# A hybrid decoder layer on one core: the last gate's first 128 channels projected inside the last stick-breaking head, a second PSUM bank for that head's values, and two products moved from GpSimd to VectorE

## The chip, the cores and the metric

The kernel runs on one core of a Trainium2 chip. The metric is the device time of one execution in microseconds (us); lower is better. The kernel before was timed in three runs: 560.47, 561.9 and 562.62 us, median 561.9.

## The reference

One layer over 1024 tokens and 1024 channels, in float32. `h` is the normalised input; one matrix product gives all projections, and three groups of heads work on their columns:

```python
proj = h @ w_in
(mu, mv, mi, mf, mz, aq, ak, av, az, sq, sk, sv, sz) = jnp.split(proj, OFFSETS, axis=-1)
y_m = mlstm_branch(...) * silu(mz)                        # 4 heads of 96, 384 columns
y_a = swa_branch(aq, ak, av, a_sinks) * silu(az)          # 6 heads of 64, 384 columns
y_s = stickbreak_branch(sq, sk, sv) * silu(sz)            # 4 heads of 64, 256 columns
y = concat([y_m, y_a, y_s]) @ w_out
x = x + gate * rmsnorm(y, g_post)
```

Stick-breaking attention, per head, for query t and keys s < t:

```python
z = q @ k.T * S_DH ** -0.5
a[t, s] = sigmoid(z[t, s]) * prod(sigmoid(-z[t, r]) for r in s+1 .. t-1)
out = a @ v
```

## The kernel before

Every float32 matrix product is made of three products of rounded parts (high by high, high by low, low by high). `hh` and `hl` hold the two parts of the transposed normalised input, 8 tiles of 128 channels by 1024 tokens. A projection of 128 channels is 48 matmuls: two halves of 512 tokens, each 3 times 8 (class `ProjD`, line 359, tile `pd<item>_<half>`). Items of this kind lie in one list, the filler. `fill(n, until)` issues the next n of its matmuls on TensorE and stops at item `until`; so the filler's matmuls stand between those of the attention stages. Items 10 to 12 are the gates `mz` (pd8 to pd10), 13 to 15 the gates `az` (pd11 to pd13), and the last four the gate `sz` of the stick-breaking heads: pd14 half 0, pd15 half 0, pd14 half 1, pd15 half 1. Each gate is multiplied with its group's output: ScalarE takes the sigmoid of the PSUM bank (L471), VectorE multiplies bank and output (L473), GpSimd multiplies in the sigmoid (L484). For `mz` and `az` the result is split in two parts and stored to DRAM (`d_yh`, `d_yl`); for `sz` it is kept in `ys`, and its split into tiles 6 and 7 of `hh`/`hl` is deferred (`late`), since the projections still read `hh`.

Order of stages, as the order on TensorE is written in the program: input, mLSTM, sliding-window attention (SWA, 8 tiles of 128 queries), stick-breaking (heads 0 to 3), the rest of the filler, the output projection. The order on the other engines is made by a scheduler at build time. Both are fixed sequences per engine: an instruction that waits holds up all behind it on its engine.

A stick-breaking head is cut in 12 pieces z (128 queries by up to 512 keys). `s_z`: TensorE writes z to one of three PSUM banks in turn (L964, L965, for the diagonal also L967), ScalarE makes sigmoid(z) into `sg` (L970) and sigmoid(-z) in place (L972), VectorE scans it to the running product `pr` (L981), and the product `sg*pr` (L983) goes to GpSimd where the piece is wider than 256, else to VectorE. A bank is free for the third piece after it when its scan has read it. `s_t` transposes the products on TensorE (L995, tile `tp`), ScalarE and VectorE split them in `ah` and `al` (L70, L71), and `s_pv`, three steps later, multiplies by the values (L1013, L1014) into one PSUM bank `ops` per four query tiles (a quad), which ScalarE and VectorE empty into `ys` (L1019, L1020). A head has 10 steps (pairs of query tiles by pairs of key tiles); after each step the filler gets 6.6 matmuls on average. In the code up to item `I_SZ` = 16, so none of `sz`.

After the last head, `wo_load(k)` loads 128 rows of the output weights (512 KB) and splits them into `woh` and `wol` (ScalarE, then GpSimd or VectorE), with two buffers for the loaded rows; `y_load(n)` loads the six stored tiles of half n over `hh`/`hl`, and the output projection goes through k = 0 to 7, for the first four token tiles (24 matmuls each k).

Of the kernel before, what the change touches and what calls it, by code (L numbers as in the profile page):

```python
# [13 lines left out]
ALU = mybir.AluOpType  # L14
# [7 lines left out]
NT = 8  # L22
# [4 lines left out]
SH = 4  # L27
# [11 lines left out]
AF_ = (4, 5, 4)  # L39
# [7 lines left out]
def trunk(ctx: ExitStack, tc, x, w_ss, w_gate, rows, cols, w_mu, w_mif, w_dm, w_av, wqk, bif, alibi, w_out,  # L47
          out):
    nc = tc.nc
    V, A, G, T = nc.vector, nc.scalar, nc.gpsimd, nc.tensor  # L50
# [12 lines left out]
    def load(dst, src):  # L63
        nc.sync.dma_start(f32(dst), f32(src))
# [3 lines left out]
    def split(dst_h, dst_l, src, e_hi, e_lo):  # L68

        e_hi(dst_h, src)  # L70
        e_lo.tensor_tensor(out=dst_l, in0=src, in1=dst_h.bitcast(F32), op=ALU.subtract)  # L71
# [41 lines left out]
    hh = hp.tile([P, KT, S], F32R, name="hh")  # L113
    hl = hp.tile([P, KT, S], F32R, name="hl")
# [331 lines left out]
        A.copy(v97[:, i, :, 0:MD], ps[:, 0:384].rearrange("p (h d) -> p h d", h=MH))  # L446
        A.copy(igf[:, :, 4 * i:4 * i + 4], ps[:, 384:392].rearrange("p (a h) -> p a h", a=2))  # L447

    late, due, clock = [], {}, [0]

    def later(n, f):

        due.setdefault(clock[0] + n, []).append(f)

    def tick():
        clock[0] += 1
        for f in due.pop(clock[0], ()):
            f()


    def from_dram(d, j):
        def src(n, t):
            z = gst.tile([P, 512], F32, tag="ymr", bufs=3, name=f"{d.name}r{j}_{n}")
            load(z, d[j, :, t])
            return z
        return src

    def gated(dst_j, name):
        def f(ps, n, t, src):
            sg = gst.tile([P, 512], F32, tag="gs", bufs=2, name=f"gs_{name}{n}")  # L470
            A.activation(sg, ps, AF.Sigmoid)  # L471
            y = src
            V.tensor_tensor(out=y, in0=ps, in1=src, op=ALU.mult)  # L473

            def rest():
                if dst_j >= 6:
                    late.append(lambda: split(hh[:, dst_j, t], hl[:, dst_j, t], y, A.copy, V))
                    return
                h = stg.tile([P, 512], F32R, tag="sh", bufs=2, name=f"sh_{name}_{n}")
                l = stg.tile([P, 512], F32R, tag="sl", bufs=2, name=f"sl_{name}_{n}")  # L480
                split(h, l, y, A.copy, G)
                store(d_yh[dst_j, :, t], h)
                store(d_yl[dst_j, :, t], l)
            later(1, lambda: G.tensor_tensor(out=y, in0=y, in1=sg, op=ALU.mult))  # L484
            later(2, rest)
        return f

    fill = Filler([ProjT(w_mif, MIF, "mif", evac_mif), ProjD(7, evac_hl(d_akh, d_akl, 0, 1.0, "ak")),
                   ProjT(w_av, AVSV, "av", evac_v)]
                  + [ProjD(4 + j, evac_hl(d_aqh, d_aql, j, 0.125, "aq")) for j in range(3)]  # L490
                  + [z for j in range(2) for z in (ProjD(j, evac_hl(d_qh, d_ql, j, 0.125, "sq")),
                                                   ProjD(2 + j, evac_hl(d_kh, d_kl, j, 1.0, "sk")))]
                  + [ProjD(8 + j, gated(j, f"mz{j}"), from_dram(d_ym, j)) for j in range(3)]
                  + [ProjD(11 + j, gated(3 + j, f"az{j}"), from_dram(d_ya, j)) for j in range(3)]
                  + [ProjD(14 + j, gated(6 + j, f"sz{j}"), lambda n, t, j=j: ys[:, j, t], halves=(n,))
                     for n in range(2) for j in range(2)])
    I_AV, I_AQ, I_SQ, I_MZ, I_SZ, I_SZ1 = 2, 3, 6, 10, 16, 18
    sstk.close()
    fill(1)

# [2 lines left out]
    for j in range(3):  # L503
# [6 lines left out]
        sg = cvp.tile([P, S], F32, tag="sg", bufs=2, name=f"cusg{j}")  # L510
# [294 lines left out]
    def bank(kind, banks, name):  # L805

        n = turn_[kind] = turn_.get(kind, -1) + 1
        return bps.tile([P, 512], F32, tag=f"b{banks[n % len(banks)]}", name=name)
# [102 lines left out]
    sh_, attn, op_t = {}, {}, {}  # L911
# [9 lines left out]
    for i in range(NT):  # L921
        if i % 2 == 0 and i + 2 < NT:
            a_load(i + 2)
        if i == NT - 2:
            fill.through(I_SQ + 2)
            s_load(0)
        nb = at_[i]["nb"]
        for n in range(4):
            if n < 3 and i + 2 < NT:
                a_z(i + 2, n)  # L930
            fill(AF_[1], I_MZ if i < NT - 1 else I_SZ)
            if i == NT - 1:
                tick()
            if n % 2 < nb:
                a_t(i, n // 2, n % 2)
                lag.append((i, n // 2, n % 2))
            if n < 2 and i + 1 < NT:
                a_exp(i + 1, range(3 * n, 3 * n + 3))
            if n == 2 and i + 1 < NT:
                a_norm(i + 1)  # L940
            if len(lag) > 3:
                a_pv(*lag.pop(0))
            if n == 2 and i + 2 < NT:
                a_max(i + 2)
# [10 lines left out]
    ys = ysp.tile([P, 2, S], F32, name="ys")  # L955
    kstk = ExitStack()
    kp = pool("kp", side="right", stack=kstk)
    def s_z(h, i, lo, nxt):

        qs, kh, kl, _ = sh_[h]  # L960
        w = min(512, (i + 1) * P - lo)
        zps = bank("z", (0, 1, 4), f"z{h}_{i}_{lo}")
        qt = qs[:, i * P:(i + 1) * P]
        T.matmul(zps[:, 0:w], qt, kh[:, lo:lo + w], start=True, stop=False)  # L964
        T.matmul(zps[:, 0:w], qt, kl[:, lo:lo + w], start=False, stop=nxt is not None)  # L965
        if nxt is None:
            T.matmul(zps[:, w - P:w], identr, mkr, start=False, stop=True)  # L967
        sg = kp.tile([P, 512], F32, tag="sg", bufs=SGB, name=f"sg{h}_{i}_{lo}")
        pr = kp.tile([P, 513], F32, tag="pr", bufs=4, name=f"pr{h}_{i}_{lo}")
        A.activation(sg[:, 0:w], zps[:, 0:w], AF.Sigmoid)  # L970

        A.activation(zps[:, 0:w], zps[:, 0:w], AF.Sigmoid, scale=-1.0)  # L972
        attn[h, i, lo // 512] = sg
        if nxt is None:
            V.memset(pr[:, w:w + 1], 1.0)
        else:
            V.tensor_copy(pr[:, w:w + 1], nxt)

        def rest():
            rev = lambda z: z[:, 0:w][:, ::-1]  # L980
            V.tensor_tensor_scan(out=rev(pr), data0=rev(zps), data1=mzero[:, 0:1].to_broadcast([P, w]),  # L981
                                 initial=1.0 if nxt is None else nxt, op0=ALU.mult, op1=ALU.add)
            (G if w > 256 else V).tensor_tensor(out=sg[:, 0:w], in0=sg[:, 0:w], in1=pr[:, 1:w + 1], op=ALU.mult)  # L983
        later(1, rest)
        return pr[:, 0:1]

# [16 lines left out]
    def s_pv(h, pair, g):  # L1003
        quad, vh = pair // 2, sh_[h][3]
        if pair % 2 == 0 and g == pair:
            op_t[h, quad] = bank("o", (5,), f"ops{h}_{quad}")
        ops = op_t[h, quad]
        ah, al = op_t.pop((h, pair, g))
        for bb in range(2):
            b = 2 * g + bb  # L1010
            c0 = P if (g == pair and bb == 1) else 0
            o = ops[:, (pair % 2) * 256 + c0:(pair % 2) * 256 + 256]
            T.matmul(o, vh[:, b, :], ah[:, bb, c0:256], start=(b == 2 * pair), stop=False)  # L1013
            T.matmul(o, vh[:, b, :], al[:, bb, c0:256], start=False, stop=(b == 1))  # L1014
        if pair % 2 == 1 and g == 0:
            p0 = (h % 2) * 64
            t = slice(quad * 512, (quad + 1) * 512)
            tmp = kp.tile([P, 512], F32, tag="otmp", bufs=1, name=f"otmp{h}_{quad}")
            A.copy(tmp[p0:p0 + 64, :], ops[64:128, :])  # L1019
            V.tensor_tensor(out=ys[p0:p0 + 64, h // 2, t], in0=ops[0:64, :], in1=tmp[p0:p0 + 64, :], op=ALU.add)  # L1020
# [21 lines left out]
    lag, total = [], 0.0  # L1042
    for s, step in enumerate(steps):
        if step[1] == 1 and step[2] == 1 and step[0] + 1 < SH:
            s_load(step[0] + 1)
        assert all(done > n for n, p in enumerate(pieces) if uses[p][0] <= s)
        s_t(*step)
        lag.append(step)
        for _ in range(SF[2]):
            if done < len(pieces) and (done < SGB or uses[pieces[done - SGB]][-1] <= s):  # L1050
                z_piece()
        total += SF[1]
        fill(int(total), I_SZ)
        total -= int(total)
        if len(lag) > SL:
            s_pv(*lag.pop(0))
        tick()
    for step in lag:
        fill(4, I_SZ)
        s_pv(*step)  # L1060
        tick()
    for _ in range(3):
# [15 lines left out]
    def y_load(n):  # L1078

        t = slice(n * 512, (n + 1) * 512)  # L1080
        for _ in range(3):
            tick()
        for z in late:
            z()
        late.clear()
        for k in range(6):
            load(hh[:, k, t], d_yh[k, :, t])
            load(hl[:, k, t], d_yl[k, :, t])
# [105 lines left out]
```

## Time and profile before

| | before |
|---|---|
| median of 3 runs | 561.9 us |
| profiled execution | 561.9 us, of which 560.0 us from the first to the last instruction (the span) |
| TensorE busy | 529.2 us, 95% |
| VectorE, ScalarE, GpSimd busy | 336.4, 250.9, 223.4 us |
| mean granted TensorE clock | 0.987 of full |

The times in the trace count from the start of the span. The SWA stage's last query tile begins at about 310 us, the first stick-breaking piece at 321 us, the last product with values ends at 442 us, the output projection begins at 464 us.

### The profile page before, as it was taken

What the parts mean: (1) busy time and instruction counts of PE and PEld (TensorE: products, weight loads), DVE (VectorE), ACT (ScalarE), POOL (GpSimd) and SP (SyncE); (2) the same over time, 40 slices, a digit from 0 to 9 for tenths busy, and PEclk for the clock granted to TensorE, in tenths of its full rate; (3) what the DMA queues carried; (4) which work ended last, traced back from release to release, by engine and by line L of the source; (5) the groups of instructions that cost most, each with busy time, mean ns of one, the idle gap of its engine ahead of it and who ended that gap; (6) DMA issues with size and microseconds to landing.
All of it is one profiled execution on the core that took longest, in us unless ns stands there. A gap on an engine that the chain in (4) does not pass through costs nothing.

```text
span 560.0 us, 8573 instructions
## 1 busy us (share of the span) xinstructions
PE 529.2 (95%) x2953; PEld 453.3 (81%) x2953; DVE 336.4 (60%) x772; ACT 250.9 (45%) x571; POOL 223.4 (40%) x208
## 2 busy tenths in 40 slices
PE   4799997999989999999999989999999899999995
PEld 3577897989968999877887778888888788888884
DVE  4686692053834778678887569777767353108232
ACT  5643443261103233338878667776676442104110
POOL 2355795430014263334453356675766252101000
PEclk9999998999979999999999999999999999999999
DMA  8981451147977465399973398365321379106421
GB/s 305 417 294 57 142 200 59 57 136 197 289 212 209 133 196 138 111 279 237 234 232 104 105 219 229 131 176 181 95 76 57 114 265 411 76 1 223 153 76 74
DMA packets 63659, 96.57 MB, mean 172 GB/s; under 512 B 17600, under 2 KB 36992, under 8 KB 63488
## 3 DMA queue, kind: packets, MB, share of 16 engines
q1 hardware_dynamic: 63616, 96.03, 54.9%
q8 instruction: 23, 0.38, 0.3%
q14 instruction: 20, 0.16, 0.1%
HBM read 69.24 MB, written 25.20 MB: 169 GB/s over the span
## 4 chain that ended last, share of the span: by engine, by line
PE 74%; DVE 11%; ACT 5%; issue 4%; POOL 3%; SPq 1%; DMA 1%; DVEq 0%; POOLq 0%; ACTq 0%
PE pd L359 24%; PE ptav L385 6%; PE mu L233 6%; PE op L1111 5%; PE op L1110 5%; PE op L1109 5%; DVE cu L507 3%; ACT zb L848 3%; PE ptmif L385 3%; PE tp L995 2%; DVE zb L858 2%; PE z L964 1%; PE mr L197 1%; PE z L965 1%; PE ops L1014 1%
## 5 line engine op out<-in xcount | busy, mean ns | idle before, releaser
L359 PE MATMUL pd<-hh,wh_d 128*128 128x512 f32 x256 | 72.3, 408 | 0.0
L359 PE MATMUL pd<-hh,wl_d 128*128 128x512 f32 x256 | 71.6, 402 | 0.0
L359 PE MATMUL pd<-hl,wh_d 128*128 128x512 f32 x256 | 70.6, 400 | 0.0
L359 PEld LDWEIGHTS pd<-hh,wh_d 128*128 128x128 f32 x256 | 47.2, 193 | 9.2 <-issue 1.0
L359 PEld LDWEIGHTS pd<-hl,wh_d 128*128 128x128 f32 x256 | 46.7, 190 | 8.4
L359 PEld LDWEIGHTS pd<-hh,wl_d 128*128 128x128 f32 x256 | 46.7, 191 | 8.3
L302 POOL TENSOR_TENSOR wl_d<-w_d,wh_d 128x512 fp32r<-128x512 f32 x32 | 46.4, 1473 | 12.6 <-ACT wh_d L300 12.6
L1109 PE MATMUL op<-woh,hh 128*128 128x512 f32 x128 | 50.6, 396 | 0.0
L1110 PE MATMUL op<-woh,hl 128*128 128x512 f32 x128 | 50.6, 396 | 0.0
L1111 PE MATMUL op<-wol,hh 128*128 128x512 f32 x128 | 50.6, 396 | 0.0
L983 POOL TENSOR_TENSOR sg<-sg,pr 128x512 f32<-128x512 f32 (+1 forms) x32 | 33.2, 1040 | 25.4 <-DVE pr L981 21.6
L71 DVE TENSOR_TENSOR al<-tp,ah 128x512 fp32r<-128x512 f32 (+2 forms) x56 | 27.6, 494 | 20.1 <-ACT ah L70 20.0
L858 POOL TENSOR_SCALAR zb<-zb,mx 128x256 f32<-128x256 f32 (+1 forms) x24 | 21.6, 913 | 41.9 <-ACT ph L70 17.0
L1122 ACT ACTIVATE sj<-op 128x512 f32<-128x512 f32 x16 | 9.5, 598 | 62.2 <-PE op L1111 59.7
L70 ACT CAST ah<-tp 128x512 fp32r<-128x512 f32 (+2 forms) x56 | 24.4, 436 | 27.7 <-PE tp L995 21.2
L1126 POOL TENSOR_TENSOR st<-st,mhalf 128x1 f32<-128x1 f32 x8 | 4.5, 556 | 68.2 <-DVE st L1125 68.2
L1110 PEld LDWEIGHTS op<-woh,hl 128*128 128x128 f32 x128 | 24.0, 188 | 5.9
L1111 PEld LDWEIGHTS op<-wol,hh 128*128 128x128 f32 x128 | 24.0, 188 | 5.8
L1109 PEld LDWEIGHTS op<-woh,hh 128*128 128x128 f32 x128 | 24.0, 188 | 5.8
L848 ACT ACTIVATE zb<-zb,mx 128x256 f32<-128x256 f32 (+1 forms) x48 | 23.2, 484 | 8.3 <-DVE mx L838 6.7
L981 DVE TENSOR_TENSOR_SCAN pr<-z,mzero 128x128 f32<-128x128 f32 (+3 forms) x32 | 25.4, 814 | 2.3 <-ACT z L972 1.9
L385 PE MATMUL ptmif<-wh_mif,hh 128*128 128x392 f32 x64 | 22.6, 353 | 3.0 <-ACT igf L447 3.0
(247 smaller groups left out, 1338.0 us busy)
## 6 DMA issues: line engine op xcount, KB each, us to landing
wm<-in_w_ss_dram SPq DMA_DIRECT2D x16, 512.0 KB, 7.7
w_d<-in_w_dm_dram SPq DMA_DIRECT2D x16, 512.0 KB, 3.7
xt<-in_x_dram SPq DMA_DIRECT2D x8, 512.0 KB, 8.1
wg<-in_w_gate_dram SPq DMA_DIRECT2D x8, 512.0 KB, 5.6
wo<-in_w_out_dram SPq DMA_DIRECT2D x8, 512.0 KB, 5.2
xr<-in_x_dram SPq DMA_DIRECT2D x8, 512.0 KB, 4.8
out_dram<-ot SPq DMA_DIRECT2D x16, 256.0 KB, 2.3
hh<-d_yh SPq DMA_DIRECT2D x12, 256.0 KB, 6.1
```

What stands on the lines that cost most here:

```text
L71: e_lo.tensor_tensor(out=dst_l, in0=src, in1=dst_h.bitcast(F32), op=ALU.subtract)
L233: T.matmul(mu_acc[j][n], w[:, cs], h[:, k, t], start=(k == 0 and w is wh and h is hh), stop=(k == KT - 1 and h is hl))
L302: G.tensor_tensor(out=wl[:, a:b], in0=z[:, a:b], in1=wh.bitcast(F32)[:, a:b], op=ALU.subtract)
L359: T.matmul(ps, w[:, k, :], h[:, k, t], start=(k == 0 and w is wh and h is hh), stop=(k == KT - 1 and h is hl))
L385: T.matmul(ps[:, 0:self.N], h[:, k, t], w[:, k % 2, :], start=(k == 0 and q == 0), stop=(k == KT - 1 and q == 2))
L848: A.activation(z, z, AF.Exp, bias=nm[:, h:h + 1], accum_out=sm[:, h:h + 1])
L858: (G if h >= 6 - NPOOL else V).tensor_scalar(out=z, in0=z, scalar1=sm[:, h:h + 1], scalar2=None, op0=ALU.mult)
L981: V.tensor_tensor_scan(out=rev(pr), data0=rev(zps), data1=mzero[:, 0:1].to_broadcast([P, w]), initial=1.0 if nxt is None else nxt, op0=ALU ...
L983: (G if w > 256 else V).tensor_tensor(out=sg[:, 0:w], in0=sg[:, 0:w], in1=pr[:, 1:w + 1], op=ALU.mult)
L1109: T.matmul(o, hh[:, k, t], woh[:, k, cs], start=(k == 0), stop=False)
L1110: T.matmul(o, hl[:, k, t], woh[:, k, cs], start=False, stop=False)
L1111: T.matmul(o, hh[:, k, t], wol[:, k, cs], start=False, stop=(k == KT - 1))
```

## The change

Five edits. (1) Item 16 is now both halves of pd14, item 17 pd15 half 0, item 18 pd15 half 1; `late` has a list for each half. (2) In the last head the filler may go on through item 16. (3) In SWA's last query tile (`i == NT - 1`) the filler gets 8 matmuls instead of 5 at each of four places. (4) The values of the last head's second quad go to bank 4, one of the three banks of z, instead of bank 5. (5) The products of pieces (0, 2) and (0, 3), 384 and 512 wide, the first two of head 0 that went to GpSimd, go to VectorE.

```diff
-    late, due, clock = [], {}, [0]
+    late, due, clock = ([], []), {}, [0]
...
-                    late.append(lambda: split(hh[:, dst_j, t], hl[:, dst_j, t], y, A.copy, V))
+                    late[n].append(lambda: split(hh[:, dst_j, t], hl[:, dst_j, t], y, A.copy, V))
...
-                  + [ProjD(14 + j, gated(6 + j, f"sz{j}"), lambda n, t, j=j: ys[:, j, t], halves=(n,))
-                     for n in range(2) for j in range(2)])
+                  + [ProjD(14 + j, gated(6 + j, f"sz{j}"), lambda n, t, j=j: ys[:, j, t], halves=hs)
+                     for j, hs in ((0, (0, 1)), (1, (0,)), (1, (1,)))])
...
+    I_SZ0 = 17
...
-            fill(AF_[1], I_MZ if i < NT - 1 else I_SZ)
+            fill(AF_[1] if i < NT - 1 else AF_[1] + 3, I_MZ if i < NT - 1 else I_SZ)
...
-            (G if w > 256 else V).tensor_tensor(out=sg[:, 0:w], in0=sg[:, 0:w], in1=pr[:, 1:w + 1], op=ALU.mult)
+            (G if w > 256 and (h > 0 or i > 3) else V).tensor_tensor(out=sg[:, 0:w], in0=sg[:, 0:w], in1=pr[:, 1:w + 1], op=ALU.mult)
...
-            op_t[h, quad] = bank("o", (5,), f"ops{h}_{quad}")
+            op_t[h, quad] = bank(f"o{quad}", (5 if h < SH - 1 or quad == 0 else 4,), f"ops{h}_{quad}")
...
-        fill(int(total), I_SZ)
+        fill(int(total), I_SZ if step[0] < SH - 1 else I_SZ0)
...
-        fill(4, I_SZ)
+        fill(4, I_SZ0)
```

TensorE in the last head, from the transposes of step (pair 3, keys 6 and 7) on; `tp` are transposes, `ops` products with values, `pd` projections. Before:

```order
L995 MATMUL tp3_3_3_4973<-ident_60,sg3_6_512_4805 128x128
L995 MATMUL tp3_3_3_4973<-ident_60,sg3_7_512_4814 128x128 x2
L1013 MATMUL ops3_1_4983<-ah3_2_2_4914,vh3_4446 128x256
L1014 MATMUL ops3_1_4983<-al3_2_2_4915,vh3_4446 128x256
L1013 MATMUL ops3_1_4983<-ah3_2_2_4914,vh3_4446 128x128
L1014 MATMUL ops3_1_4983<-al3_2_2_4915,vh3_4446 128x128
```

The same place now:

```order
L997 MATMUL tp3_3_3_5004<-ident_60,sg3_6_512_4824 128x128
L997 MATMUL tp3_3_3_5004<-ident_60,sg3_7_512_4833 128x128 x2
L359 MATMUL pd14_0_4940<-hl_99,wh_d14_4724 128x512 x7
L1015 MATMUL ops3_1_5025<-ah3_2_2_4926,vh3_4469 128x256
L1016 MATMUL ops3_1_5025<-al3_2_2_4927,vh3_4469 128x256
L1015 MATMUL ops3_1_5025<-ah3_2_2_4926,vh3_4469 128x128
L1016 MATMUL ops3_1_5025<-al3_2_2_4927,vh3_4469 128x128
```

Seven projection matmuls now stand ahead of the first product of the second quad, and 0 to 7 ahead of each later group; all 48 of pd14 are issued before the last products, and 48 of pd15 are left after them.

VectorE at the beginning of head 0; `pr` are scans, `sg` products, `al` low parts of transposed products, `d_ym...r` gate products. Before:

```order
L981 SCALAR_TENSOR_TENSOR pr0_2_0_3543<-z0_2_0_3538,mzero_65 128x384
L975 MEMSET pr0_5_512_3611 128x1
L473 TENSOR_TENSOR d_ym_91r0_1_3458<-pd8_1_3460,d_ym_91r0_1_3458 128x512
L981 SCALAR_TENSOR_TENSOR pr0_3_0_3569<-z0_3_0_3564,mzero_65 128x512
L71 TENSOR_TENSOR al0_0_0_3592<-tp0_0_0_3587,ah0_0_0_3591 128x256
L981 SCALAR_TENSOR_TENSOR pr0_4_512_3602<-z0_4_512_3597,mzero_65 128x128
```

Now:

```order
L983 SCALAR_TENSOR_TENSOR pr0_2_0_3570<-z0_2_0_3565,mzero_65 128x384
L977 MEMSET pr0_5_512_3628 128x1
L985 TENSOR_TENSOR sg0_2_0_3569<-sg0_2_0_3569,pr0_2_0_3570 128x384
L983 SCALAR_TENSOR_TENSOR pr0_3_0_3592<-z0_3_0_3587,mzero_65 128x512
L985 TENSOR_TENSOR sg0_3_0_3591<-sg0_3_0_3591,pr0_3_0_3592 128x512
L71 TENSOR_TENSOR al0_0_0_3609<-tp0_0_0_3604,ah0_0_0_3608 128x256
L983 SCALAR_TENSOR_TENSOR pr0_4_512_3619<-z0_4_512_3614,mzero_65 128x128
```

The two products stand directly behind their scans; the gate product of pd8's second half has moved ahead of all scans.

The queue of SyncE, which issues the DMAs, behind the last head; `wo` are output weights, `hh` and `hl` the stored tiles. Before:

```order
L64 DMA wo0_5056<-in_w_out_dram 128x1024
L64 DMA wo1_5060<-in_w_out_dram 128x1024
L64 DMA hh_98<-d_yh_93 128x512
L64 DMA wo2_5064<-in_w_out_dram 128x1024
L64 DMA wo3_5068<-in_w_out_dram 128x1024
L64 DMA hh_98<-d_yh_93 128x512
L64 DMA hl_99<-d_yl_94 128x512 x2
```

Now:

```order
L64 DMA wo0_5121<-in_w_out_dram 128x1024
L64 DMA wo1_5125<-in_w_out_dram 128x1024
L64 DMA hh_98<-d_yh_93 128x512 x3
L64 DMA hl_99<-d_yl_94 128x512 x3
```

Three tiles of `hh` and three of `hl` now stand ahead of the third tile of weights.

## Rows read from the trace of the kernel before

**Rows 1.** The page's head and the row of part 1 (busy us, share of the span, instructions of each engine).

```profile
span 560.0 us, 8573 instructions
PE 529.2 (95%) x2953; PEld 453.3 (81%) x2953; DVE 336.4 (60%) x772; ACT 250.9 (45%) x571; POOL 223.4 (40%) x208
```

**Rows 2.** Busy time of each engine by stretch: stretch, its length, busy us (instructions) of TensorE, weight loads, VectorE, ScalarE, GpSimd, then granted clock, DMA share, GB/s.

```profile
310.00:320.00 10.00, 10.00 (x54) 8.57 (x54) 5.41 (x12) 6.25 (x14) 2.10 (x2) 1.00 0.44 145
330.00:340.00 10.00, 8.16 (x35) 6.44 (x34) 7.95 (x16) 5.67 (x14) 6.45 (x6) 0.83 1.01 272
340.00:350.00 10.00, 10.00 (x62) 8.78 (x61) 9.73 (x23) 7.73 (x19) 6.74 (x7) 1.00 0.76 188
360.00:420.00 60.00, 59.88 (x360) 52.58 (x359) 45.68 (x95) 43.19 (x98) 38.90 (x34) 1.00 0.42 128
430.00:440.00 10.00, 8.40 (x59) 7.15 (x58) 5.70 (x12) 5.12 (x11) 5.07 (x5) 1.00 0.20 79
...
430.00:446.00 16.00, 14.40 (x92) 12.39 (x91) 7.55 (x14) 6.39 (x14) 5.07 (x5) 1.00 0.31 108
```

**Rows 3.** TensorE's waits, for 305 to 345 us (first row) and 418 to 466 us (second): engine and line, who was waited for, us in total, times, longest.

```profile
PE tp L995 <- POOL sg L983: 1.8, 1, 1.8
...
PE ops L1013 <- DVE ys L1020: 1.5, 1, 1.5
```

**Rows 4.** The first stall and what follows, by single microseconds; columns as in rows 2.

```profile
333.00:334.00 1.00, 1.00 (x5) 0.81 (x6) 0.61 (x4) 0.37 (x1) 1.00 (x1) 0.62 0.90 196
334.00:335.00 1.00, 1.00 (x4) 0.81 (x3) 0.20 (x1) 0.81 (x2) 0.26 (x1) 0.50 1.19 211
335.00:336.00 1.00, 1.00 (x4) 0.79 (x3) 0.69 (x1) 1.00 (x3) 0.00 (x0) 0.50 1.23 297
336.00:337.00 1.00, 1.00 (x4) 0.78 (x3) 0.96 (x3) 0.47 (x2) 0.33 (x1) 0.67 1.13 390
```

**Rows 5.** Timeline around the first stall: start, duration, engine, line, operation, tiles, shapes, count, and the idle time before it with its releaser. VectorE's scan of piece (0, 3); GpSimd's low parts of the next gate's weights and its product of piece (0, 3); TensorE's transposes of pieces (0, 2) and (0, 3).

```profile
328.74 1.22 DVE L981 TENSOR_TENSOR_SCAN pr<-z,mzero 128x512 f32<-128x512 f32 x1 [1.06 <-ACT z L972]
329.22 2.52 POOL L302 TENSOR_TENSOR wl_d<-w_d,wh_d 128x512 fp32r<-128x512 f32 x2
331.71 1.13 POOL L983 TENSOR_TENSOR sg<-sg,pr 128x512 f32<-128x512 f32 x1
330.79 0.27 PE L995 MATMUL tp<-ident,sg 128*128 128x128 f32 x1
332.89 0.33 PE L995 MATMUL tp<-ident,sg 128*128 128x128 f32 x1 [1.83 <-POOL sg L983]
```

**Rows 6.** Timeline, products on VectorE beside work on GpSimd: two with GpSimd idle, then two beside GpSimd's work of rows 5, then one at 355.38 with GpSimd's instruction.

```profile
323.88 0.29 DVE L983 TENSOR_TENSOR sg<-sg,pr 128x128 f32<-128x128 f32 x1
324.81 0.43 DVE L983 TENSOR_TENSOR sg<-sg,pr 128x256 f32<-128x256 f32 x1
331.11 0.79 DVE L983 TENSOR_TENSOR sg<-sg,pr 128x128 f32<-128x128 f32 x1
331.88 1.24 DVE L983 TENSOR_TENSOR sg<-sg,pr 128x256 f32<-128x256 f32 x1
355.38 1.45 DVE L983 TENSOR_TENSOR sg<-sg,pr 128x256 f32<-128x256 f32 x1
355.16 1.39 POOL L484 TENSOR_TENSOR d_ym_91r<-d_ym_91r,gs_mz 128x512 f32<-128x512 f32 x1
```

**Rows 7.** VectorE from the scan of piece (0, 3) to the end of the scan of the 11th piece, (0, 6) keys 0 to 511: the stretch as in rows 2, that scan, and TensorE's matmul of the 14th piece, (1, 1), which takes the same bank.

```profile
328.74:343.86 15.12, 13.29 (x67) 10.88 (x65) 12.96 (x23) 10.09 (x25) 10.67 (x10) 0.89 0.84 225
342.58 1.27 DVE L981 TENSOR_TENSOR_SCAN pr<-z,pr,mzero 128x512 f32<-128x512 f32 x1
344.19 0.34 PE L964 MATMUL z<-kh,qs 128*128 128x256 f32 x1
```

**Rows 8.** The second stall: TensorE's timeline in the last head, and the chain of waits (start, us, what) for the 96 matmuls of `sz` behind it.

```profile
435.02 0.49 PE L995 MATMUL tp<-ident,sg 128*128 128x128 f32 x3
437.01 0.39 PE L1013 MATMUL ops<-ah,vh 128*128 128x256 f32 x1 [1.51 <-DVE ys L1020]
...
442.35 21.77 PE pd L359 x96
464.12 0.23 PE op L1109
```

**Rows 9.** Behind the last head: the DMA queue's issues (start, us), ScalarE's and GpSimd's split of the first weights, and the time from issue to landing of the `hh` loads.

```profile
442.38 1.72 SPq L64 DMA_DIRECT2D wo<-in_w_out_dram  x2
449.87 0.33 SPq L64 DMA_DIRECT2D hh<-d_yh  x1
458.77 0.32 SPq L64 DMA_DIRECT2D hl<-d_yl  x1
445.90 1.05 ACT L70 CAST woh<-wo 128x1024 fp32r<-128x1024 f32 x1 [2.88 <-DMA wo<-in_w_out_dram]
447.03 2.42 POOL L71 TENSOR_TENSOR wol<-wo,woh 128x1024 fp32r<-128x1024 f32 x1 [7.42 <-ACT woh L70]
DMA to landing us min/median/max: 3.0/6.1/6.6
```

More of the change, by code (lines that the diff above doesn't have):

```diff
@@ L1082, in y_load @@
             tick()
-        for z in late:
+        for z in late[n]:
             z()
-        late.clear()
         for k in range(6):
```

## The prediction

> **What bounds the kernel now.** I read the page's first part first: TensorE is busy 529.2 of 560.0 us [rows 1], so a change that adds no matmuls and removes none can win only where TensorE stands still or runs slowly. Next, the busy time by stretches shows where that is in the part that the change touches [rows 2]: from 310 to 320 us and from 340 to 350 TensorE is full, from 360 to 420 it misses 0.12 us of 60, but from 330 to 340 it has 8.16 of 10 and a granted clock of 0.83, and from 430 to 440 it has 8.40 of 10. The table of waits names both holes [rows 3]: one transposition waits 1.8 us for GpSimd's product, and one product with values waits 1.5 us for VectorE to empty the `ops` bank. Everywhere else in these stages a matmul that is moved merely changes places with another.
>
> The first hole costs twice. TensorE stops at 331.06 and goes on at 332.89 [rows 5], and then the granted clock is 0.62, 0.50, 0.50 and 0.67 of full in the four microseconds that follow [rows 4], that is, the lower of its two levels (1.2 instead of 2.4 GHz) for most of them. The work lost to the clock is 0.38 + 0.50 + 0.50 + 0.33 = 1.71 us, so this hole costs 1.83 + 1.71 = 3.54 us. The second costs its time alone: the clock stays at 1.00 [rows 2].
>
> **The change part by part, on the trace's time** (561.9 us, of which 1.9 lie outside the span; it is also the median, so one subtraction serves for both).
>
> *Products of pieces (0, 2) and (0, 3) to VectorE.* Why does TensorE wait at 331? VectorE's scan of piece (0, 3) is over at 328.74 + 1.22 = 329.96, but GpSimd is then inside 2.52 us of weight splitting which stand ahead of the product in its order, so that the product runs only from 331.71 to 332.84 [rows 5]. On VectorE the product follows its scan at once. Its price there is not shown for this width; the narrower ones take 0.29 us (128 wide) and 0.43 (256 wide) with GpSimd idle [rows 6], so 0.14 for each 128, and 0.57 and 0.71 us for 384 and 512 as my estimate. The scan's end plus 0.71 is 330.67, just before TensorE wants it (330.79 in the old spacing). The 1.83 us go, and with them I expect the drop of the clock to go, since the other hole, 1.51 us long, was followed by none [rows 2, 8].
>
> What is late next is VectorE. It is busy 9.73 of the 10 us after the stall [rows 2]; the stall gave it time to catch up. The bank of the 11th piece must be scanned before the 14th piece's matmul can write it, and that scan ended at 343.85, 0.34 us before the matmul at 344.19 [rows 7]. So TensorE cannot be earlier there by more than VectorE is earlier, plus 0.34. From the scan of (0, 3) to that point VectorE needed 15.12 us, 12.96 of them busy [rows 7]. Now the 2.16 idle us can close up, since TensorE no longer holds the pieces back; one product of 0.71 joins (the other lies before the stretch); and 0.5 + 0.8 us of the busy time were two narrow products stretched by GpSimd's work (0.79 us against 0.29 and 1.24 against 0.43 [rows 6]), which may or may not come back. That is 12.96 + 0.71 = 13.67 us, or 12.4 without the stretching: 1.45 to 2.8 us earlier, with the slack 1.8 to 3.1. From this I take off some 0.4 us, because in the new order ScalarE's gate sigmoid and a weight cast, and VectorE's gate product, stand ahead of the first pieces and delay the first scans. I take 2.0 us of the 3.54 as the gain; the rest comes back as several short waits of `z` for a bank. The bounds are 0 (VectorE takes the whole stall over) and 3.54. Behind this place TensorE was full with VectorE at 7 to 8 tenths (45.68 of 60 us in 360 to 420 [rows 2]), so the lead that is left there should last.
>
> A rule of the Trainium skill (SBUF — State Buffer, "Who interferes with whom") speaks against this edit: VectorE's second SBUF read port is GpSimd's too, it is locked for a whole instruction, and an instruction of VectorE with two SBUF inputs is shut out while GpSimd reads SBUF. The trace agrees: a 256-wide product takes 0.43 us alone but 1.24 and 1.45 us beside GpSimd, and ends 0.2 to 0.3 us after GpSimd's instruction does. Its result is a rival below.
>
> *Three more matmuls at four places of SWA's last tile.* TensorE is full there [rows 2], so the 12 matmuls cost 12 x 0.227 = 2.7 us at that place and save as much later: 0. They bring the weight splitting that blocked GpSimd forward by the same 2.7 us, which helps the first edit, and they use up filler that the next edit replaces.
>
> *pd14 into the last head, and bank 4.* Behind the last head 96 matmuls of `sz` take 21.77 us, 0.227 each [rows 8]; 48 of them, 10.9 us, now lie inside it. TensorE still has to do them, so the gain is the idle time that they fill: in 430 to 446 us TensorE is busy 14.40 of 16.00 [rows 2], 1.6 us, of which 1.51 is the wait for the `ops` bank [rows 8]. With a second bank this wait disappears, and seven matmuls (1.6 us) stand in front of it besides; either alone would be nearly enough. Bank 4 was last used by a piece z that is scanned long before. The gate's evacuation (ScalarE, VectorE, GpSimd) is not new work; it moves into a stretch where VectorE is busy 5.70 of 10 us and ScalarE 5.12 [rows 2], and costs nothing while TensorE has filler. I take 1.6 us, between 1.0 (a short wait left at the head's end) and 1.9.
>
> *The cover behind the last head is halved.* From the last product to the output projection there were 21.8 us; now 10.9. Needed by then: the first weights split (GpSimd done at 447.03 + 2.42 = 449.45, 7.1 us after the first issue at 442.38) and `hh`, `hl` of k = 0. Their loads were issued first at 449.87, 7.5 us behind [rows 9], because they waited for TensorE's last reading of `hh` and stood partly behind weights that waited for a buffer. Now the last reading of half 0's first `hh` tile is the ninth matmul of pd15, 9 x 0.227 = 2.0 us behind the head, and the queue has three `hh` and three `hl` directly behind two weight tiles; `hl`'s first is read at 17 x 0.227 = 3.9. With the median 6.1 us to landing [rows 9] they are there at 8.1 and 10.0, before 10.9. After that a k lasts 24 matmuls, 5.6 us, and wants one weight tile, which ScalarE (1.05) and GpSimd (2.42) or VectorE prepare faster. I cost this at 0; if the cover fails it is the third rival.
>
> Sum: 2.0 + 1.6 = 3.6 us; 561.9 - 3.6 = **558.3 us**.
>
> **The rivals.**
> 1. *The lock.* If both moved products meet an instruction of GpSimd, each loses up to 1.3 us (the weight halves take 2.52/2 = 1.26 [rows 5]); 2.6 us late on a full VectorE eats the 2.0 and 0.6 more: 561.9 - 1.6 + 0.6 = 560.9. For it: rows 6. Against: in the new order GpSimd's weight splitting lies earlier by 2.7 us and should be over before the second product.
> 2. *No new wait at all.* VectorE keeps up, and the whole 3.54 + 1.6 = 5.1 us come off: 556.8. For it: VectorE's 2.16 idle us and the stretched products. Against: the slack of 0.34 us.
> 3. *The output projection waits: slower.* The place is its first matmul; the point, whether `hh` or `hl` of k = 0 lands later than 10.9 us behind the head. If the loads are issued as late as before (7.5 us) they land at 13.6, 2.7 us too late, with the clock's loss of 1.7 a stall of 4.4: 558.3 + 4.4 = 562.7. If the whole half had to be loaded first (last issue at 458.77, 16.4 us behind, landing at 22.5), it is 11.6 us: 569.9. For it: landing takes up to 6.6 us with weights in the same queue. Against: the new order of that queue.
>
> **How the numbers follow.** Forecast 0.58, the lock 0.15, no new wait 0.17, the late output 0.10. The forecast's own range is 557.2 to 559.8, from the bounds of its two terms taken about half. Leaving out half of the second rival's lower side and most of the third's, 8 of 10 lie within 556.4 and 561.4. A measurement of this kernel tells 0.5%, 2.8 us, from no change: faster means below 559.1, slower above 564.7. Faster: 0.45 of the forecast's 0.58 and all of 0.17, 0.62; slower: half of the third, with a little for what I have not seen, 0.06; within: 0.32.
>
> **What would show it.** The waits of transpositions for GpSimd's product should be gone at head 0, with the clock at 1.00 in the ten microseconds behind; VectorE should be above 9.5 of 10 us there, and short waits of `z` for the scan appear, some 1.5 us in sum. The wait of `ops` for `ys` in the last head's middle should be gone, and TensorE full from there to the output. pd's matmuls behind the last head should last 10.9 us, with no gap before the first `op`, and the output phase should be as long as before. Wrong would be: a stall at head 0 of over a microsecond in one piece with a low clock behind it (the lock), or a gap before the first `op`.

## The result and the profile after

The changed kernel took 556.66 us (median of 5 runs, 555.57 to 557.74) against 561.25 us for the kernel before on the same chip (560.46 to 562.62). The ratio is 0.9924, with a 95% interval from 0.9906 to 0.9942: faster by 0.8%, where 558.3 us was forecast. The profiled execution took 556.66 us too, with a span of 554.9 (before 560.0). The page's head and its first part, answering to [rows 1]:

```profile
span 554.9 us, 8574 instructions
PE 527.5 (95%) x2953; PEld 452.3 (82%) x2953; DVE 336.3 (61%) x774; ACT 250.5 (45%) x571; POOL 222.4 (40%) x206
```

TensorE has the same 2953 matmuls; two products moved from GpSimd (208 to 206) to VectorE (772 to 774). Whatever came off the time was idle or slow TensorE: of the 5.1 us of span, 1.7 are busy time (529.2 to 527.5, matmuls that no longer run at the low clock) and 3.4 idle time. Busy time by stretch, columns as in [rows 2]:

```profile
330.00:340.00 10.00, 10.00 (x55) 8.14 (x53) 9.83 (x22) 8.38 (x22) 6.21 (x6) 1.00 1.05 301
340.00:350.00 10.00, 10.00 (x60) 8.79 (x60) 9.74 (x23) 8.85 (x20) 7.54 (x8) 1.00 0.85 216
360.00:420.00 60.00, 59.64 (x358) 52.20 (x357) 47.36 (x96) 41.80 (x96) 36.77 (x33) 1.00 0.40 123
430.00:440.00 10.00, 9.98 (x60) 8.47 (x59) 5.52 (x11) 4.60 (x10) 4.19 (x4) 1.00 0.14 54
```

Both holes are closed: 330 to 340 us has 10.00 busy instead of 8.16 and a granted clock of 1.00 instead of 0.83, and 430 to 440 has 9.98 instead of 8.40. VectorE at head 0 is as full as forecast (9.83 of 10), and TensorE doesn't wait for it; the short waits of `z`, some 1.5 us in sum, that the prediction expected there did not come. The waits of TensorE, two from 305 to 345 us and one from 345 to 470 us, answer to [rows 3]:

```profile
PE atp L867 <- DVE pl L71: 0.5, 2, 0.3
PE ao L883 <- DVE ya L896: 0.4, 1, 0.4
...
PE ops L1015 <- DVE ys L1022: 0.4, 1, 0.4
```

The first two lie in SWA, ahead of 310 us, and stood in the kernel before too; neither the wait of `tp` for GpSimd nor the 1.5 us of `ops` is left. The timeline at head 0, answering to [rows 5 to 7], by engine: VectorE's products and scans, GpSimd, and TensorE's first `z`, the three transposes of pieces (0, 2) and (0, 3), which now run without a stall, and the 14th and 16th `z`:

```profile
330.34 0.67 DVE L985 TENSOR_TENSOR sg<-sg,pr 128x384 f32<-128x384 f32 x1
330.93 1.21 DVE L983 TENSOR_TENSOR_SCAN pr<-z,mzero 128x512 f32<-128x512 f32 x1
332.24 0.69 DVE L985 TENSOR_TENSOR sg<-sg,pr 128x512 f32<-128x512 f32 x1
341.84 1.28 DVE L983 TENSOR_TENSOR_SCAN pr<-z,pr,mzero 128x512 f32<-128x512 f32 x1
...
327.81 2.79 POOL L302 TENSOR_TENSOR wl_d<-w_d,wh_d 128x512 fp32r<-128x512 f32 x2
330.55 1.60 POOL L71 TENSOR_TENSOR sl_mz<-d_ym_91r,sh_mz 128x512 fp32r<-128x512 f32 x1
...
323.70 0.22 PE L966 MATMUL z<-kh,qs 128*128 128x128 f32 x1
333.33 0.49 PE L997 MATMUL tp<-ident,sg 128*128 128x128 f32 x3
343.51 0.33 PE L966 MATMUL z<-kh,qs 128*128 128x256 f32 x1
346.57 0.45 PE L966 MATMUL z<-kh,qs 128*128 128x512 f32 x1
```

From the first `z` to the 14th TensorE now needs 343.51 - 323.70 = 19.81 us; before it needed 344.19 - 321.16 = 23.03. Two things in the rows are new. The 512-wide product takes 0.69 us on VectorE, as estimated (0.71). And GpSimd's two weight halves, which blocked its product before, are over at 330.60, that is 6.9 us behind the first `z`; before they were over at 331.74, 10.6 us behind it [rows 5]. Which of the two closed the hole, this trace alone can't say.

Behind the last head (DMA queue, then GpSimd, then TensorE), answering to [rows 8, 9]:

```profile
448.13 1.72 SPq L64 DMA_DIRECT2D wo<-in_w_out_dram  x2
450.18 1.27 SPq L64 DMA_DIRECT2D hh<-d_yh  x3
451.99 1.43 SPq L64 DMA_DIRECT2D hl<-d_yl  x3
...
453.25 2.40 POOL L71 TENSOR_TENSOR wol<-wo,woh 128x1024 fp32r<-128x1024 f32 x1 [3.37 <-ACT woh L70]
...
447.94 1.99 PE L359 MATMUL pd<-hh,wh_d 128*128 128x512 f32 x8
458.82 0.40 PE L1110 MATMUL op<-woh,hh 128*128 128x512 f32 x1
```

The first `hh` load of these and the first `hl` load by themselves (size, us from issue to landing):

```profile
hh<-d_yh SPq DMA_DIRECT2D x1, 256.0 KB, 5.4
hl<-d_yl SPq DMA_DIRECT2D x1, 256.0 KB, 6.0
```

`pd15` begins at 447.94; the first `hh` load is issued 2.2 us behind that and the first `hl` load 4.1 us (reckoned 2.0 and 3.9), the weights are split 7.7 us behind (reckoned 7.1), and the output projection begins 10.88 us behind, without a gap. The first `hh` tile has landed 7.6 us behind and the first `hl` tile 10.05 us (reckoned 8.1 and 10.0); `hl` is first read at 459.06, 11.1 us behind, so 1.1 us were to spare. The output projection lasts 554.9 - 458.82 = 96.1 us, before 560.0 - 463.96 = 96.0.

### The profile page after: what moved, and what is told of

Read it like the earlier page. It is cut to its first block, busy times and chain, and to the rows that moved or that the text cites. A ratio compares the mean times of both kernels' runs of the same rounds, so it can differ in the third digit from the quotient of the medians.

```text
span 554.9 us, 8574 instructions
## 1 busy us (share of the span) xinstructions
PE 527.5 (95%) x2953; PEld 452.3 (82%) x2953; DVE 336.3 (61%) x774; ACT 250.5 (45%) x571; POOL 222.4 (40%) x206
## 4 chain that ended last, share of the span: by engine, by line
PE 80%; DVE 10%; ACT 5%; issue 2%; POOL 1%; DMA 1%; DVEq 0%; POOLq 0%; SPq 0%; ACTq 0%
PE pd L359 26%; PE ptav L385 6%; PE mu L233 6%; PE op L1112 5%; PE op L1111 5%; PE op L1110 5%; PE ptmif L385 3%; PE tp L997 3%; DVE cu L509 3%; ACT zb L850 3%; PE ops L1016 2%; PE ops L1015 2%; DVE zb L860 2%; PE z L966 2%; PE xps L166 2%
## 5 line engine op out<-in xcount | busy, mean ns | idle before, releaser
L985 POOL TENSOR_TENSOR sg<-sg,pr 128x512 f32<-128x512 f32 (+1 forms) x30 | 31.1, 1041 | 19.7 <-DVE pr L983 19.4
```

The source lines that it names most:

```text
L985: (G if w > 256 and (h > 0 or i > 3) else V).tensor_tensor(out=sg[:, 0:w], in0=sg[:, 0:w], in1=pr[:, 1:w + 1], op=ALU.mult)
```

## The experiments

Two stretches are compared in every run, both read from TensorE's timeline. A goes from the first to the 16th `z` of head 0. B goes from there to the first `op`; where the filler drew 12 matmuls ahead of A (17 in the last two rows), 0.227 us each is added back, so that all runs but e8_cover, which leaves matmuls out, have the same work in B. Before, A is 347.27 - 321.16 = 26.11 us and B 116.69; the times have their own runs of the kernel before on the same chip, so ratios are compared. A and B are those of one profiled execution each. Of these, only before and e7_pd14 ran at the low clock behind the stall at head 0 (some 1.7 us); e4_bank has the same stall without it.

| run | edits in it | median, us | ratio (95% interval) | A | B |
|---|---|---|---|---|---|
| before | none | 561.25 | 1 | 26.11 | 116.69 |
| the change | 1 to 5 | 556.66 | 0.9924 (0.9906 to 0.9942) | 22.87 | 114.97 |
| e1_prod | 5 | 560.47 | 0.9997 (0.9982 to 1.0013) | 24.96 | 116.68 |
| e2_fill | 3 | 559.6 | 0.9989 (0.9978 to 0.9999) | 22.93 | 118.17 |
| e4_bank | 4 | 559.76 | 0.9999 (0.9978 to 1.002) | 24.82 | 116.34 |
| e7_pd14 | 1, 2 | 559.18 | 0.9973 (0.9954 to 0.9992) | 26.08 | 114.63 |
| e3_noprod | all but 5 | 556.66 | 0.9928 (0.9904 to 0.9951) | 22.92 | 114.92 |
| e5_nobank | all but 4 | 556.63 | 0.9922 (0.9898 to 0.9946) | 22.86 | 114.92 |
| e6_nofill | all but 3 | 557.71 | 0.9945 (0.9925 to 0.9965) | 24.08 | 114.64 |
| e9_min | 1, 2, 3 | 556.68 | 0.9922 (0.9897 to 0.9947) | 22.93 | 114.93 |
| e8_cover | 1 to 5, 16 matmuls left out | 557.5 | 0.9942 (0.9919 to 0.9964) | 22.86 | 112.71 |
| e10_more | 1 to 5, more of 3 | 558.12 | 0.9947 (0.9925 to 0.9968) | 24.47 | 116.40 |
| e11_more_noprod | 1 to 4, more of 3 | 556.33 | 0.9919 (0.9897 to 0.9941) | 22.63 | 116.35 |

The theory from the prediction was that the product's engine (edit 5) closes the hole at head 0. The rival, from the rows after, was that the earlier weight splitting (edit 3) does.

**The products alone (e1_prod).** The kernel before with edit 5:

```diff
-            (G if w > 256 else V).tensor_tensor(out=sg[:, 0:w], ...
+            (G if w > 256 and (h > 0 or i > 3) else V).tensor_tensor(out=sg[:, 0:w], ...
```

> Edit 5 alone: the products of pieces (0, 2) and (0, 3) on VectorE, everything else as before. Measure besides the time: the stretch from the first matmul of the first gate item (pd8) to the first of the output projection, 153.96 us before, 149.05 after, and the stall of the transposition in head 0 (1.83 us before, none after). Theory A (the product's engine makes the stall): no stall, full clock behind it, stretch shorter by about 3.2 us (150.8). Theory B (GpSimd's weight splitting, at 329.2 to 331.7 us, makes it, wherever the product is: on VectorE it is shut out until GpSimd's instruction ends): the product ends at about 332, the transposition stalls for about 1.1 us, and the stretch is shorter by 0.7 us if the clock falls all the same (153.2), by 2.4 if it does not (151.5).

The timeline at head 0: a scan, VectorE's product of piece (0, 3) behind it, GpSimd's second weight half beside it, and the transposes that waited:

```profile
330.31 0.41 DVE L981 TENSOR_TENSOR_SCAN pr<-z,mzero 128x128 f32<-128x128 f32 x1
330.64 1.80 DVE L983 TENSOR_TENSOR sg<-sg,pr 128x512 f32<-128x512 f32 x1
330.62 1.28 POOL L302 TENSOR_TENSOR wl_d<-w_d,wh_d 128x512 fp32r<-128x512 f32 x1
332.50 0.44 PE L995 MATMUL tp<-ident,sg 128*128 128x128 f32 x2 [1.32 <-DVE sg L983]
```

The hole is still 1.3 us; it has only changed the engine that it waits for. The product no longer stands behind the weight halves in GpSimd's queue, but it runs beside them, and there it is shut out: it takes 1.80 us where it takes 0.69 in the change, and TensorE goes on at 332.50, after GpSimd's halves end at 331.90. This is the prediction's first rival, the lock, in the place given, but for one of its two products: that of piece (0, 2), at 327.72, took 0.55 us. The time doesn't differ from that of before. A is 1.15 us shorter than in the trace of before, but no shorter than in e4_bank (24.82), which has the old stall at full clock: what A gained here is the clock.

**The three more matmuls alone (e2_fill).**

```diff
-            fill(AF_[1], I_MZ if i < NT - 1 else I_SZ)
+            fill(AF_[1] if i < NT - 1 else AF_[1] + 3, I_MZ if i < NT - 1 else I_SZ)
```

> Edit 3 alone: 12 more filler matmuls in SWA's last tile, products on GpSimd as before. Theory A: the stall stays at 1.0 to 1.8 us with its clock, stretch 153 to 154. Theory B: the weight splitting is over some 2.7 us earlier relative to head 0, GpSimd's product of (0, 3) ends about when TensorE wants it, stall at most 0.4 us, no drop of the clock, 3.2 us saved; the filler runs dry 12 matmuls earlier in the last head, which may give back up to 1 us there: stretch 150.8 to 151.8.

TensorE's waits, at head 0 (first row) and behind it:

```profile
PE tp L995 <- POOL sg L983: 0.2, 1, 0.2
...
PE ops L1013 <- DVE ys L1020: 2.6, 3, 1.4
```

The busy time of two stretches of the last head:

```profile
420.00:430.00 10.00, 9.10 (x52) 7.55 (x50) 8.24 (x16) 7.12 (x16) 7.48 (x8) 1.00 0.14 52
430.00:440.00 10.00, 8.34 (x65) 7.56 (x66) 5.95 (x11) 4.94 (x10) 3.11 (x3) 1.00 0.14 54
```

With the product still on GpSimd the hole shrinks from 1.8 to 0.2 us, and A to 22.93, within 0.1 us of the whole change. GpSimd's halves are over 6.9 us behind the first `z` (330.06 against 323.17), as in the change. Of the 3.7 us that they are earlier, 2.7 are the 12 matmuls; besides, the scheduler has put the product of piece (0, 2) behind the halves. Whether the matmuls alone would do in the old order was not tested. An edit costed at 0 carries the first term. But the 12 matmuls that it draws ahead are missing later: with the filler's limit unchanged, the last head runs out of filler, its holes are 2.56 us in the two stretches instead of 1.60, B is 1.5 us longer, and the time moves by a tenth of a per cent only.

**pd14 in the last head alone (e7_pd14), and the bank alone (e4_bank).** The first is the changed kernel without edits 3 to 5; the second is the kernel before with this line:

```diff
-            op_t[h, quad] = bank("o", (5,), f"ops{h}_{quad}")
+            op_t[h, quad] = bank(f"o{quad}", (5 if h < SH - 1 or quad == 0 else 4,), f"ops{h}_{quad}")
```

> Edits 1 and 2 alone (pd14 inside the last head; no second bank, no extra filler, products as before). Second hole closed (TensorE 9.9 or more of 10 us from 430 to 440), first hole as before with its 1.83 us: stretch 152.3 if the clock falls behind it, 150.6 if not; time 558.3 to 559. If the halved cover behind the last head cost anything, a gap before the first matmul of the output projection.

> Edit 4 alone: the second bank for the last head's second quad, no projection moved. If the wait for the bank is all of the second hole: its 1.5 us go, stretch 152.4. If without filler another wait takes its place (the transposed products through ScalarE and VectorE, three steps behind): 0 to 0.8 us saved, stretch 153.2 to 154.

Busy time in e7_pd14 at head 0 and in the last head:

```profile
330.00:340.00 10.00, 8.16 (x37) 6.44 (x36) 7.84 (x16) 5.66 (x14) 6.11 (x7) 0.83 0.95 258
430.00:440.00 10.00, 9.98 (x60) 8.50 (x59) 4.92 (x10) 4.32 (x9) 4.61 (x4) 1.00 0.18 66
```

The same of e4_bank:

```profile
330.00:340.00 10.00, 8.16 (x43) 6.53 (x41) 8.71 (x17) 7.16 (x18) 6.62 (x6) 1.00 0.93 256
430.00:440.00 10.00, 8.49 (x65) 7.85 (x64) 5.27 (x9) 5.18 (x10) 3.10 (x3) 1.00 0.21 80
```

TensorE's two longest waits in e4_bank, at head 0 and in the last head:

```profile
PE tp L995 <- POOL sg L983: 1.8, 1, 1.8
...
PE tp L995 <- DVE al L71: 1.5, 1, 1.5
```

The filler alone closes the hole in the last head and leaves the one at head 0 as it was, low clock included; B falls by 2.06 us. The bank alone removes its wait, and another of 1.5 us, of the transposes for VectorE's `al`, stands in its place. e4_bank is 1.3 us shorter than before in A, which has no cause in the edit: the stall at head 0 is the same 1.8 us, but the clock behind it is 1.00, not 0.83.

**The whole change without one part (e3_noprod, e5_nobank, e6_nofill), and the smallest set (e9_min).** Each is the changed kernel with one of the lines above as it was before: the product's, the bank's, the three matmuls'. e9_min has the lines of the product and of the bank as before.

> The changed kernel without edit 5 (products of head 0 on GpSimd again). Theory A: the stall is back, stretch 149.05 + 3.2 = 152.2, time about 559.8. Theory B: a stall of at most 0.4 us, stretch 149.1 to 149.5, time as the changed kernel's (about 557).

> The changed kernel without edit 4 (one bank for the last head's values). If the moved projection is what closes the second hole: the seven matmuls ahead of the second quad cover the emptying of the bank, wait at most 0.5 us, stretch (first matmul of pd8 to the first of the output projection) 149.0 to 149.5, time as the changed kernel's, about 556.7. If the bank is needed: a wait of 1.0 us or more there, stretch 150 or more.

> The changed kernel without edit 3 (5 filler matmuls again in SWA's last tile). Theory B (GpSimd's weight splitting must be early): the stall of about 1.3 us is back in head 0, as with edit 5 alone, stretch 150.0 to 150.5 at full clock, 1.7 more if the clock falls; time 557.7 to 559. Theory A (the product's engine decides): no stall, 149.05 and 556.7.

> The kernel before with the reordered filler (edits 1 and 2) and the three more matmuls (edit 3); the bank and the two products as before. My theory: these three edits are the whole change, since each of the other two was found to change nothing beside them. From the first matmul of pd8 to the first of the output projection 149.0 us as with the whole change (before 153.96), time about 556.7. Rival, that the bank and the products each cover for the other (either alone suffices but not neither): the wait of tp for GpSimd's product or of ops for ys is back at 1 us or more, 150 to 151 us, time about 558.

GpSimd in e3_noprod at head 0, and the transposes that wait for its last product:

```profile
328.53 2.78 POOL L302 TENSOR_TENSOR wl_d<-w_d,wh_d 128x512 fp32r<-128x512 f32 x2
331.26 1.28 POOL L71 TENSOR_TENSOR sl_mz<-d_ym_91r,sh_mz 128x512 fp32r<-128x512 f32 x1
332.49 1.93 POOL L985 TENSOR_TENSOR sg<-sg,pr 128x384 f32<-128x384 f32 x2
334.47 0.44 PE L997 MATMUL tp<-ident,sg 128*128 128x128 f32 x2 [0.16 <-POOL sg L985]
```

The halves are over 6.9 us behind the first `z` here too (331.31 against 324.42), GpSimd gets to both products in time, and TensorE waits 0.16 us. A and B of e3_noprod, e5_nobank and e9_min are those of the whole change within 0.1 us: beside edits 1 to 3, the products and the bank do nothing that can be measured. Without edit 3, with the products on VectorE (e6_nofill), two short waits come back at head 0 (0.2 us for a product, 0.5 us for a scan), not the one stall of 1.3 us that was expected, and A is 1.2 us longer. At head 0 this kernel has the same edit as e1_prod, and again the product of (0, 3) and the second weight half begin within 0.02 us of each other; but here the half is the one that waits:

```profile
329.33 0.67 DVE L985 TENSOR_TENSOR sg<-sg,pr 128x512 f32<-128x512 f32 x1
329.32 1.82 POOL L302 TENSOR_TENSOR wl_d<-w_d,wh_d 128x512 fp32r<-128x512 f32 x1
```

So without edit 3, what the products gain hangs on a near tie, which they lost in e1_prod (1.80 and 1.28 us) and won here (0.67 and 1.82). They don't stand in for the three more matmuls; beside those they are not needed.

**The cover behind the last head, made shorter (e8_cover).** The change with a third of the matmuls of `pd15`'s second half:

```diff
-                for w, h in ((wh, hh), (wl, hh), (wh, hl)):
+                passes = ((wh, hh), (wl, hh), (wh, hl))[:1 if (self.ti, n) == (15, 1) else 3]
+                for m, (w, h) in enumerate(passes):
```

> The changed kernel with 16 of the 24 matmuls of pd15's second half left out (its low parts; that gate of half 1 is then only of rounded parts). The cover behind the last head shrinks from 10.9 to 7.3 us. If the loads behind the last head set the start of the output projection as reckoned (weights' low part 7.7 us behind, hl 9 to 11 us behind), TensorE waits 1.5 to 3.5 us there, and the time is 556.7 - 3.6 + 2.5 = 555.6 (554.6 to 556.6, and up to 1.7 more if the clock falls). If the cover was still ample: no wait, 553.1.

Among the matmuls left out are the last that read half 1 of `hl`, and the queue changes too: six `hl` loads are now issued ahead of the weights. TensorE's part of the head ends at 447.20. The loads, and the first two `op`, in the timeline:

```profile
443.90 2.69 SPq L64 DMA_DIRECT2D hl<-d_yl  x6
455.85 0.48 PE L1111 MATMUL op<-woh,hh 128*128 128x512 f32 x1 [1.23 <-DMA hh<-d_yh]
457.95 0.55 PE L1112 MATMUL op<-woh,hl 128*128 128x512 f32 x1 [1.62 <-DMA hl<-d_yl]
```

The busy time behind them:

```profile
458.00:460.00 2.00, 2.00 (x5) 1.57 (x6) 2.00 (x3) 0.62 (x1) 1.26 (x1) 0.57 1.01 353
460.00:462.00 2.00, 2.00 (x7) 1.57 (x6) 1.01 (x2) 0.00 (x0) 1.51 (x1) 0.58 1.01 352
```

`hh` is there 8.65 us behind the head and `hl` 10.75 us (reckoned 8.1 and 10.0; 7.6 and 10.05 in the change, where the six loads are not ahead of them). With 3.6 us less work in front of them, TensorE waits 2.85 us and then runs at a clock of 0.57 and 0.58, some 0.43 x 2 + 0.42 x 2 = 1.7 us more; the run is no faster than the change. So the third rival's mechanism is real, and the change stays clear of it by the 1.1 us of above. How much of the wait here is the shorter cover and how much the six loads, this run can't say.

**More filler ahead of head 0 (e10_more), and the same with the products on GpSimd (e11_more_noprod).** In the changed kernel TensorE still misses 1.3 of 10 us from 300 to 310 us, where the item limit cuts the filler short. The edit gives it five matmuls more at one place of the tile before the last (the expectation of e11_more_noprod speaks of three places):

```diff
-            fill(AF_[1] if i < NT - 1 else AF_[1] + 3, I_MZ if i < NT - 1 else I_SZ)
+            fill(AF_[1] if (i, n) < (NT - 2, 3) else AF_[1] + 3, I_MZ if (i, n) < (NT - 2, 3) else I_SZ)
```

> The whole change, and the filler's last place in SWA's tile before the last one gets 8 matmuls too and may take them from the next gate (before: 5, of which the limit let 3 through). If TensorE's hole just ahead of 310 us (0.7 us in 308 to 310) is filled by them and nothing else moves: 0.7 us faster than the whole change, about 556.0. Rival: the five matmuls are then missing at the end of the last head, where the filler of the whole change is all used, and about the same 0.7 to 1.1 us comes back there as waits of ops, z or tp: 556.7, no difference.

> The run before this one (three more places of the filler ahead of head 0), with the two products back on GpSimd. My theory: that run lost what it had gained because VectorE's product of piece (0, 3) was shut out by GpSimd's gate product beside it (1.64 us instead of 0.69) and TensorE stood 1.6 us; on GpSimd the product stands in one queue with the gate product and can't be shut out by it, so the hole at head 0 is at most 0.5 us and 0.6 us remain as gain over the whole change: about 556.1. Rival: in GpSimd's own queue the product now waits behind the weight splitting or the gate product, tp waits 1 us or more for GpSimd, and the time is 557 to 558 as in that run.

VectorE, GpSimd and TensorE in e10_more at head 0:

```profile
332.82 1.26 POOL L484 TENSOR_TENSOR d_ym_91r<-d_ym_91r,gs_mz 128x512 f32<-128x512 f32 x1 [3.54 <-DVE d_ym_91r L473]
332.99 1.64 DVE L985 TENSOR_TENSOR sg<-sg,pr 128x512 f32<-128x512 f32 x1
334.69 0.44 PE L997 MATMUL tp<-ident,sg 128*128 128x128 f32 x2 [1.61 <-DVE sg L985]
```

GpSimd at the same place in e11_more_noprod:

```profile
330.75 0.87 POOL L985 TENSOR_TENSOR sg<-sg,pr 128x384 f32<-128x384 f32 x1 [1.23 <-DVE pr L977]
331.89 1.09 POOL L985 TENSOR_TENSOR sg<-sg,pr 128x512 f32<-128x512 f32 x1 [0.28 <-DVE pr L983]
```

TensorE's one kind of wait in e11_more_noprod behind 345 us:

```profile
PE ops L1015 <- DVE ys L1022: 1.3, 3, 0.6
```

In e10_more the filler moves the gate product to the same moment as VectorE's product: a product that takes 0.69 us alone takes 1.64, and TensorE stands for 1.61. With the product in GpSimd's own queue it runs right behind its scan, ahead of the gate product, and that stall is gone. So edit 5 is not only idle beside edit 3; in another order it costs a stall of 1.6 us. What e11_more_noprod wins ahead of head 0 (9.44 us busy from 300 to 310 instead of 8.74) it gives back behind, where the filler is now short and `ops` waits three times (B 1.4 us longer than with the change): 556.33 us, no measurable gain. The waits of `ops` that e10_more's rival expected are there in both runs (1.1 us in e10_more); its time, no difference, holds for e11_more_noprod, while e10_more has the stall at head 0 besides.

## Why the prediction was right, and where it was not

*What bounds the kernel.* Right: TensorE gained only where it stood or ran slowly, and moved matmuls changed places.

*First term, 2.0 us: carried by another edit.* The step "on VectorE the product follows its scan at once", by which the products were to remove the stall, failed: e1_prod shows the lock in its place. The step that cost edit 3 at 0 failed with it. It is nothing as work, and everything as a shift: the prediction saw that it brings the weight splitting forward, and counted that as help. That the first term came out at all is luck as far as its step goes: edit 3, which removed the stall, was part of the same change.

Its size depends on the clock. Against the trace of before A fell by 26.11 - 22.87 = 3.24 us; against e4_bank's A, with the stall at full clock, by 24.82 - 22.87 = 1.95. The term took the low clock as part of the stall, and that came in some executions only; of the 3.54 us only 1.83 were certain. The part held back for VectorE did not come back: from the scan of (0, 3) to the end of the 11th piece's, VectorE took 343.12 - 330.93 = 12.19 us (12.4 to 13.67 reckoned), since the two stretched products did not recur, and it began 7.23 us behind the first `z`, not later than before (7.58) as the 0.4 assumed. So the second rival's size was right for an execution with the low clock.

*Edits 1, 2 and 4, 1.6 us: right.* e6_nofill and e7_pd14 gain 2.05 and 2.06 us in B, the whole change 1.72. The remark that bank or filler would each be nearly enough was half right: the filler is enough, the bank is not.

*The cover at 0: right in its result and in its steps*: in the change `hh` landed 0.5 us earlier than reckoned and `hl` as reckoned. The margin was 1.1 us.

*The sum.* In the two traces A and B together gave 3.24 + 1.72 = 4.96 us instead of 3.6, and without the low clock it would be 1.95 + 1.72 = 3.67. By the ratio of the runs the change is worth 0.76% of 561.25, 4.3 us, between the two. How many executions of the kernel before had the low clock there is not recorded. Of the 1.6 us between forecast and result, 0.65 is the kernel before itself, whose median moved from 561.9 (three runs) to 561.25 (five). The result lies below the forecast's own range (557.2 to 559.8) and within the wide one.

## What to carry to other kernels

When one engine waits for another's instruction, look at what stands ahead of that instruction in its queue, and try first to move that in time; changing the engine can leave the wait in place under a new name, as with the products. A part that is free as work can carry the change through what it shifts, and what it draws ahead is missing later: edit 3 was worth a tenth of a per cent until edits 1 and 2 refilled the place that it emptied. Test a set of edits by leaving one out and by the smallest set, not by parts alone: the four parts alone gave 0.03, 0.11, 0.01 and 0.27%, the smallest set and the whole both 0.8%.

## What the runs showed of the hardware

The same stall was followed by the low clock in some executions and not in others. After 1.83 us without matmuls the clock fell to about half in the kernel before [rows 4] and in e7_pd14 (0.83 over the ten microseconds); in e4_bank, with the same 1.8 us, it stayed at 1.00, as it did after 1.3 us in e1_prod and 1.6 us in e10_more. After the two waits of e8_cover it fell to 0.57. The ten microseconds with the stall in e1_prod, then in e10_more:

```profile
330.00:340.00 10.00, 8.45 (x42) 6.41 (x41) 9.86 (x20) 7.43 (x18) 6.22 (x6) 1.00 1.01 273
330.00:340.00 10.00, 8.38 (x47) 6.89 (x46) 9.93 (x20) 7.52 (x20) 4.01 (x4) 1.00 1.07 287
```

What decides it at this length stays open.

VectorE and GpSimd delay each other in both directions. VectorE's 512-wide product takes 0.69 us alone, 1.64 us beside the gate product of e10_more and 1.80 us beside the weight half of e1_prod. In the changed kernel the 384-wide product began first (330.34), and GpSimd's low-part instruction that began beside it at 330.55 took 1.60 us where it takes 1.28 in e3_noprod; in e6_nofill a weight half took 1.82 us instead of 1.28. The Trainium skill (SBUF — State Buffer, "Who interferes with whom") states that the two engines share a read port that is locked for a whole instruction; these durations agree with it, in both directions.
